# Four tiles of the per-layer embedding computed during the routing, the other four at the end of the expert stage

## The chip, the cores and the metric

The kernel runs on one core of a Trainium2 chip. Its time is the device time of one launch in microseconds (us). Three runs of the kernel before took 1029.37 to 1033.73 us, median 1030.36. The trace was taken in a further, profiled execution of the same kernel, which took 1031.45 us.

## The reference

One layer of a hybrid network on 1024 tokens of width 1024, in float32. The part that the change touches is what follows the mixers: the output projection, a mixture of 32 experts of which every token uses two, and an embedding that is added for each layer.

```python
x = x + jnp.concatenate([attn_out, ml_out], axis=-1) @ w_o[i]
x = x + _hier_moe(_rmsnorm(x, norm_ffn_g[i]), w_router_group[i], ..., w_gate_e[i], w_up_e[i], w_down_e[i])
hp = _rmsnorm(x, norm_ple_g[i])
x = x + (p[i] @ w_ple[i]) * jax.nn.sigmoid(hp @ w_ple_gate[i])
return _rmsnorm(x, final_norm_g)
...
def expert(args):                      # for the rows that the routing sent to expert e
    xb, e = args
    return (jax.nn.silu(xb @ w_g[e]) * (xb @ w_u[e])) @ w_d[e]
```

`p[i]` is 1024 x 256 and `w_ple` 256 x 1024. Their product, the per-layer embedding, depends on nothing that the layer computes, so that it can be made at any time before the last stage. In rows of 128 tokens it has eight tiles.

## The kernel before

Every large product is made from three products of rounded parts: a weight or activation is split into a high part (ScalarE copies it, rounding it) and a low part (VectorE subtracts), and `mm3` (L127 to L129) adds high x high, high x low and low x high. A split of 128 x 1024 elements thus takes one ScalarE and one VectorE instruction (L132, L133).

The stages in order are the mixers (up to about 430 us of the span), the output projection with the router's logits for eight row tiles (`out_tile`), the rest of the routing, the expert stage (`experts`), an overflow loop for experts with over 128 rows, and the final stage (gate by `w_ple_gate`, sum, norm).

In the output projection TensorE makes `wops` (the projection), transposes the result (`h2p`) and multiplies by the router's weights (`rps`). The sum x goes to `x2d` and the normalised rows go to `h2d` in DRAM, both on GpSimd's DMA queue. After the last tile comes what is called the gap of the routing here: counts (`cnt`), positions and two tables (`tab`) are worked out by VectorE and TensorE in turn, until the list `gidx` (L1017) tells which rows each expert takes. GpSimd then gathers the rows of the first two experts (L1149) into two buffers `xg` that ScalarE has filled before (L1200).

In the expert stage each step e gathers rows for expert e + 2, transposes and splits those of e + 1 (`xgp`, `xh`, `xl`), loads the weights of e + 3, multiplies expert e by its gate and up weights (`gups`, 24 matmuls of 128 x 512 in two halves), finishes e - 1 (transposes `ehp`, split `eht`, 12 + 12 matmuls `eyps`, eviction `ey`, scatter to `ybd`), and splits the weights of e + 1 and e. Each expert has two loads `rgu` for each half of gate and up (512 KB each) and one `rdn` of 1024 KB for down. They are issued by SyncE, in order, into a ring of nine raw buffers (4 KB or 8 KB a partition); a load waits until what stood in its buffer has been split. Split weights go into a second ring of buffers W.

A tile of the embedding (`ple_tile`) is two transposes `pps` of its input `pin`, a split of 128 x 256, twelve matmuls `pleps` of 128 x 512 and two evictions `pley`. Six tiles are made in the steps 14, 16, 18, 20, 22 and 24 (`PLE_AT`, L1235), in buffers of the raw ring that are given up for them (`retire`), one 8 KB buffer for two tiles. The weights `w_ple` are loaded in step 5 and split in steps 7 and 9. The seventh tile is made in `final_load`, ahead of the overflow loop, while the gate's weights `rpg` are loaded and split, and the eighth in `final`, after that loop. Instructions are ordered within an engine by a scheduler that takes priority, by place in the program, and dependences; each engine then runs its own list in order, and a semaphore wait holds up all that stands behind it on that engine.

Of the kernel before, what the change touches and what calls it, by code (L numbers as in the profile page):

```python
# [10 lines left out]
F32 = mybir.dt.float32  # L11
F32R = mybir.dt.float32r
# [8 lines left out]
P = 128  # L21
# [15 lines left out]
MLPRI = 800  # L37
PLE_LOAD = 5
PLE_W = (7, 9)
PLE_AT = (14, 16, 18, 20, 22, 24)  # L40
MAGIC = 12582912.0
# [18 lines left out]
class Kernel:  # L60
# [64 lines left out]
    def mm3(self, out, w_hi, w_lo, m_hi, m_lo, start, stop):  # L125
        nc = self.nc
        nc.tensor.matmul(out, w_hi, m_hi, start=start, stop=False)  # L127
        nc.tensor.matmul(out, w_hi, m_lo, start=False, stop=False)  # L128
        nc.tensor.matmul(out, w_lo, m_hi, start=False, stop=stop)  # L129

# [734 lines left out]
    def out_tile(self, i, gb, before):  # L865
# [14 lines left out]
        def mm(c, lo_k, hi_k):  # L880
            s = slice(c * 512, (c + 1) * 512)
            for k in range(lo_k, hi_k):
                self.mm3(ps[c], hi[:, k], lo[:, k], self.wo[k][:, 0, s], self.wo[k][:, 1, s], k == 0, k == KT - 1)

# [318 lines left out]
    def experts(self, gu3):  # L1203
        col = lambda t, e: t[:, e:e + 1]
        xg = [self.moe_gather(col(self.gidx, e)) for e in range(2)]
        with self.tc.issue_after(self.gathered.ins):
            self.raws[3] = gu3, self.load_gu(3, 1, self.nc.gpsimd), self.load_dn(3)
        x, gu, h, dn = {0: self.moe_x(xg[0])}, {0: self.first[0]}, {}, {0: self.first[1]}
        for e in range(N_EXP + 1):
            if e + 2 < N_EXP:  # L1210
                xg.append(self.moe_gather(col(self.gidx, e + 2)))
            if e + 1 < N_EXP:
                x[e + 1] = self.moe_x(xg[e + 1])
            if 4 <= e + 3 < N_EXP:
                self.raws[e + 3] = self.moe_load(e + 3)
            if e < N_EXP:
                h[e] = self.moe_gu(x.pop(e), gu.pop(e))
            if e:
                self.moe_y(h.pop(e - 1), dn.pop(e - 1), col(self.sidx, e - 1))
            if e + 1 < N_EXP:  # L1220
                with self.tc.issue_after(self.routed.ins):
                    gu[e + 1] = self.split_gu(self.raws[e + 1][:2])
            if 0 < e < N_EXP:
                dn[e] = self.split_w(self.raws.pop(e)[2:])
            if e == 4:
                with self.tc.issue_after(self.last_split[1]):
                    self.route_over()
                self.close("RT")
                self.open("PL", "right")
            if e == PLE_LOAD:  # L1230
                self.ple_load()
            if e in PLE_W:
                self.ple_weights(PLE_W.index(e))
            if e in PLE_AT:
                self.ple_tile(PLE_AT.index(e))  # L1235
            if e + 1 in PLE_AT[1:]:
                self.ple_in(PLE_AT.index(e + 1))

# [15 lines left out]
    def final_load(self):  # L1254
# [5 lines left out]
        raws = [self.R("rpg") for _ in range(4)]  # L1260
        for i in range(len(PLE_AT), NT):
            self.ple_in(i)
# [4 lines left out]
        with self.tc.issue_after(sa), self.tc.issue_after(sv):  # L1267
            self.wring, self.nw = wr, 0
            self.wgs = self.split_gate(raws[:1], 0)
            self.ple_tile(len(PLE_AT))  # L1270
            self.wgs += self.split_gate(raws[1:3], 2)
        self.rest = wr, raws[3:]
        self.fin = {}
# [5 lines left out]
    def ple_load(self):  # L1279
        self.plew = []  # L1280
        self.ple_raw = [self.ple_half(0)]
        self.pin, self.pw = {}, {}
        self.ple_in(0)

# [16 lines left out]
    def ple_tile(self, i):  # L1301
# [6 lines left out]
        py = self.po2("pleps")  # L1308
        n = i - len(PLE_AT)
        if n >= 0:  # L1310
            y = self.t("B", "pley", [P, D], bufs=2, tag="ey") if n % 2 else self.t("B", "pley", [P, D], tag=f"xg{n // 2 % 2}")
        else:
            if i % 2 == 0:
                pool, tag = self.retire()
                self.ples = self.t(pool, "ples", [P, 2 * D], tag=tag)
            y = self.ples[:, i % 2 * D:(i % 2 + 1) * D]
        for c in range(2):
# [50 lines left out]
    def final(self):  # L1368
# [5 lines left out]
        with self.tc.issue_after(self.fin[0][2].ins):  # L1374
# [5 lines left out]
            self.final_in(1)  # L1380
        rest = list(range(len(PLE_AT) + 1, NT))
        with ExitStack() as st:
# [39 lines left out]
    def run(self):  # L1422
# [13 lines left out]
        for i in range(NT):  # L1436
            end = self.out_tile(i, gb, end)
            if i == 1:
                self.raws[0] = self.moe_load(0)
            if i == 4:  # L1440
                list(self.route_tiles(0, 4))
                self.first = self.split_gu(self.raws[0][:2]), self.split_w(self.raws[0][2:])
            if i == 5:
                self.raws[1] = self.moe_load(1)
        rt = self.route_tiles(4, 7)
        next(rt)
        end()
        list(rt)
        gu2 = self.load_gu(2, 0)
        self.close("A3")  # L1450
# [3 lines left out]
        self.open("B", "left")  # L1454
        self.rring, self.nr = [("R2", f"R{i}") for i in range(4, 9)] + [self.rring[(self.nr + i) % 4] for i in range(4)], 0
        more = [("B", f"W{i}") for i in range(6, 9)]
        self.wring += more[:NW - 6]
        self.rring[5:5] = more[NW - 6:]
        self.raws[2] = gu2, self.load_gu(2, 1), self.load_dn(2)
        self.moe_setup()  # L1460
# [40 lines left out]
```

## Time and profile before

| | |
|---|---|
| median of 3 runs | 1030.36 us (1029.37 to 1033.73) |
| profiled execution | 1031.45 us, span 1029.7 us, mean granted TensorE clock 0.966 |
| TensorE (PE) busy | 953.9 us, 93% of the span |
| VectorE (DVE) busy | 805.8 us, 78% |
| ScalarE (ACT) busy | 666.7 us, 65% |
| SyncE's and ScalarE's DMA queue (q1) | 146.00 MB, 42.4% of 16 engines' span |
| GpSimd's DMA queue (q0) | 38.33 MB, 10.4% |

The span runs from the first to the last instruction; the shares are means over stages that differ much. The output projection runs from about 433 us, the gap from about 545 to 567, the experts up to about 909 and the final stage from 916. "PEclk" is the granted clock of TensorE, 1.00 being 2.4 GHz and 0.50 being 1.2 GHz. A release in brackets, as [5.77 <-DVE M L967], says how long the engine had been idle before the instruction and what ended that.

### The profile page before, as it was taken

How to read it: one execution, taken by the hardware profiler on the slowest of the kernel's cores; microseconds unless marked ns; L12 is line 12 of the kernel's file. 1: busy time of each engine (PE TensorE's matmuls, PEld its weight loads, DVE VectorE, ACT ScalarE, POOL GpSimd, SP SyncE). 2: the span in 40 equal slices, each digit the busy share in tenths (PEclk: the TensorE clock that was granted, in tenths of full speed). 3: DMA queues.
4: the chain of work that ended last, by engine and by line, in shares of the span. 5: the costliest groups of instructions: out<-in, count | busy, mean ns of one | idle time of the engine just before them, and what ended most of it. 6: DMA issues, size and time to landing. Idle time of an engine off the chain costs nothing. (4 is left out here: it accounts for less than half of the span.)

```text
span 1029.7 us, 16040 instructions
## 1 busy us (share of the span) xinstructions
PE 953.9 (93%) x5583; PEld 819.2 (80%) x5583; DVE 805.8 (78%) x1877; ACT 666.7 (65%) x1182; POOL 165.7 (16%) x213
## 2 busy tenths in 40 slices
PE   4999999998999999899995989999699999979996
PEld 4999999996788888688884867888588888858875
DVE  7759788367888989774747899998678889858885
ACT  5554766254788889763333877998578788755432
POOL 4000000101222322101013121222112112210000
PEclk9999999999999999899996998999899999989999
DMA  7230111310000001698348898999999999774541
GB/s 220 101 101 25 42 62 59 102 37 11 17 11 14 13 12 23 229 295 288 123 159 272 261 359 283 354 351 343 338 301 315 341 304 356 243 254 173 184 164 61
DMA packets 127360, 185.36 MB, mean 180 GB/s; under 512 B 19487, under 2 KB 105070, under 8 KB 123182
## 3 DMA queue, kind: packets, MB, share of 16 engines
q1 hardware_dynamic: 111502, 146.00, 42.4%
q0 software_dynamic: 15776, 38.33, 10.4%
q8 instruction: 44, 0.72, 0.3%
q14 instruction: 38, 0.31, 0.1%
HBM read 167.48 MB, written 33.59 MB: 195 GB/s over the span
## 5 line engine op out<-in xcount | busy, mean ns | idle before, releaser
L133 DVE TENSOR_TENSOR w<-rgu,w 128x1024 fp32r<-128x1024 f32 x128 | 155.1, 1227 | 32.8 <-ACT w L132 29.6
L132 ACT ACTIVATE w<-rgu 128x1024 fp32r<-128x1024 f32 x128 | 133.3, 1065 | 6.1 <-PE gups L129 3.3
L127 PE MATMUL inp<-hh,win 128*128 128x256 f32 x384 | 111.7, 291 | 0.0
L129 PE MATMUL inp<-hh,win 128*128 128x256 f32 x384 | 111.1, 290 | 0.5 <-DVE win L256 0.5
L128 PE MATMUL inp<-hl,win 128*128 128x256 f32 x384 | 111.4, 291 | 0.1
L127 PE MATMUL gups<-w,xh 128*128 128x512 f32 x256 | 103.8, 405 | 0.0
L128 PE MATMUL gups<-w,xh 128*128 128x512 f32 x256 | 102.0, 398 | 0.0
L129 PE MATMUL gups<-w,xl 128*128 128x512 f32 x256 | 101.2, 395 | 0.0
L133 DVE TENSOR_TENSOR w<-rdn,w 128x1024 fp32r<-128x1024 f32 x64 | 77.2, 1219 | 2.7 <-ACT w L132 1.9
L129 PEld LDWEIGHTS inp<-hh,win 128*128 128x128 f32 x384 | 74.6, 195 | 0.7 <-DVE win L256 0.7
L128 PEld LDWEIGHTS inp<-hl,win 128*128 128x128 f32 x384 | 74.6, 194 | 0.5 <-DVE hl L133 0.4
L127 PEld LDWEIGHTS inp<-hh,win 128*128 128x128 f32 x384 | 74.5, 194 | 0.3 <-ACT z L331 0.2
L132 ACT ACTIVATE w<-rdn 128x1024 fp32r<-128x1024 f32 x64 | 66.0, 1067 | 4.1 <-PE gups L129 3.7
L1149 POOL DMA_INDIRECT xg<-h2d,gidx x32 | 37.1, 1159 | 179.2 <-PE xgp L1159 145.8
L1188 ACT ACTIVATE ey<-eyps 128x512 f32<-128x512 f32 x64 | 38.2, 596 | 40.4 <-PE eyps L129 30.8
L705 PE MATMUL po<-pt,V 128*128 128x256 f32 x320 | 61.2, 307 | 0.9 <-ACT pt L132 0.5
L133 DVE TENSOR_TENSOR pt<-ptp,pt 128x512 fp32r<-128x512 f32 (+2 forms) x112 | 54.3, 491 | 7.3 <-ACT pt L132 5.7
L132 ACT ACTIVATE pt<-ptp 128x512 fp32r<-128x512 f32 (+2 forms) x112 | 48.1, 443 | 14.7 <-PE ptp L693 7.4
L127 PE MATMUL eyps<-w,eht 128*128 128x512 f32 x128 | 54.5, 426 | 2.4 <-ACT eht L132 2.3
L129 PEld LDWEIGHTS gups<-w,xl 128*128 128x128 f32 x256 | 48.3, 189 | 9.5
L128 PEld LDWEIGHTS gups<-w,xh 128*128 128x128 f32 x256 | 48.6, 190 | 9.1
L127 PEld LDWEIGHTS gups<-w,xh 128*128 128x128 f32 x256 | 48.7, 190 | 9.0 <-ACT xh L132 0.2
(392 smaller groups left out, 2633.2 us busy)
## 6 DMA issues: line engine op xcount, KB each, us to landing
rdn<-in_w_down_e_dram SPq DMA_DIRECT2D x32, 1024.0 KB, 8.9
rgu<-in_w_gate_e_dram SPq DMA_DIRECT2D x62, 512.0 KB, 11.5
rgu<-in_w_up_e_dram SPq DMA_DIRECT2D x62, 512.0 KB, 10.0
wraw<-in_w_in_dram SPq DMA_DIRECT2D x11, 512.0 KB, 5.4
x<-in_x_dram SPq DMA_DIRECT2D x8, 512.0 KB, 4.6
abw<-mlrows SPq DMA_DIRECT2D x8, 512.0 KB, 3.7
mixf<-mixd SPq DMA_DIRECT2D x8, 512.0 KB, 5.7
xres<-in_x_dram SPq DMA_DIRECT2D x8, 512.0 KB
```

The source lines that it names most:

```text
L127: nc.tensor.matmul(out, w_hi, m_hi, start=start, stop=False)
L128: nc.tensor.matmul(out, w_hi, m_lo, start=False, stop=False)
L129: nc.tensor.matmul(out, w_lo, m_hi, start=False, stop=stop)
L132: a = self.nc.scalar.activation(hi, src, AF.Copy)
L133: v = self.nc.vector.tensor_sub(lo, src, hi)
L705: nc.tensor.matmul(po, self.V[kt][:, h, :], pts[t - 1][:, w, u, :], start=(kt + w == 0), stop=(kt == 2 * j + 1 and w == 1))
L1149: self.gathered = self.nc.gpsimd.indirect_dma_start(out=xg, out_offset=None, in_=self.h2d, in_offset=bass.IndirectOffsetOnAxis(ap=gcol, ax ...
L1188: nc.scalar.activation(y[:, s], py[c], AF.Copy)
```

## The change

Four tiles (0 to 3) are made in the gap: `w_ple` (1 MB) and the four inputs (512 KB) are loaded during the output projection and the weights are split there, in buffers of the ring W; the products are evicted to buffers of the projection stage and stored to `pled` in DRAM by ScalarE's queue, one 512 KB store a tile. SyncE loads them again in steps 26 and 28, two tiles a load. Tiles 4 and 5 are made in `final_load`, tiles 6 and 7 in `final`; the weights are loaded a second time from step 20 on and split in steps 22 and 24. Further, expert 0's down weights are split in step 0 rather than in the projection, and expert 1's down load and all of expert 2's loads come after the projection's buffers are closed. `mm3` returns its last instruction, after which the early tiles may be issued, at a priority behind the routing.

```diff
-PLE_LOAD = 5
-PLE_W = (7, 9)
-PLE_AT = (14, 16, 18, 20, 22, 24)
+PLE_LOAD = 20
+PLE_W = (22, 24)
+N_EARLY = 4
+PLE_BACK = (26, 28)
...
-        x, gu, h, dn = {0: self.moe_x(xg[0])}, {0: self.first[0]}, {}, {0: self.first[1]}
+        x, gu, h, dn = {0: self.moe_x(xg[0])}, {0: self.first}, {}, {}
...
+            if e == 0:
+                with self.tc.issue_after(self.routed.ins):
+                    dn[0] = self.split_w(self.raws.pop(0)[2:])
...
-            if e in PLE_AT:
-                self.ple_tile(PLE_AT.index(e))
-            if e + 1 in PLE_AT[1:]:
-                self.ple_in(PLE_AT.index(e + 1))
+            if e in PLE_BACK:
+                self.ple_back(PLE_BACK.index(e))
...
+            self.ple_tile(N_EARLY)
             self.wgs += self.split_gate(raws[1:3], 2)
+            self.ple_tile(N_EARLY + 1)
...
+    def early_in(self):
+
+        raw = self.R("rple")
+        self.nc.sync.dma_start(raw, self.a["w_ple"][0].rearrange("(p k) n -> p (k n)", k=2))
+        self.early_w = raw
+
+    def early_p(self):
+        t = self.R("pins")
+        self.early_x = t.rearrange("p (i n) -> p i n", n=DE)
+        self.nc.sync.dma_start(self.early_x[:, 0:N_EARLY], self.a["p"][0, 0, 0:N_EARLY * P, :].rearrange("(i p) n -> p i n", p=P))
+
+    def early_split(self):
+        self.early_w = self.split_w([self.early_w])
+        self.pled = self.t("dr", "pled", [N_EARLY * P, D])
+
+    def early_tile(self, i):
+        nc = self.nc
+        pt = self.pT("pps")
+        for k in range(2):
+            nc.tensor.transpose(pt[:, k, :], self.early_x[:, i, k::2], self.ident)
+        ht = self.t("A3", "pht", [P, 2, 2, P], F32R, 2, "mixl")
+        self.split(ht[:, 0], ht[:, 1], pt[:, 0:2])
+        py = self.po2("pleps")
+        y = self.t("A3", "pley", [P, D], F32, 2, "mixh") if i % 3 else self.t("A3", "pley", [P, D], tag="mixf")
+        w = self.early_w
+        for c in range(2):
+            s = slice(c * 512, (c + 1) * 512)
+            for k in range(2):
+                self.mm3(py[c], ht[:, 0, k], ht[:, 1, k], w[k][0][:, s], w[k][1][:, s], k == 0, k == 1)
+            nc.scalar.activation(y[:, s], py[c], AF.Copy)
+        nc.scalar.dma_start(self.pled[i * P:(i + 1) * P, :], y)
+
+    def ple_back(self, n):
+        pool, tag = self.retire()
+        t = self.t(pool, "ples", [P, 2, D], tag=tag)
+        self.nc.sync.dma_start(t, self.pled[2 * n * P:2 * (n + 1) * P, :].rearrange("(i p) n -> p i n", p=P))
+        for i in range(2):
+            self.pw[2 * n + i] = t[:, i]
...
+            if i == 0:
+                self.early_in()
             if i == 1:
                 self.raws[0] = self.moe_load(0)
+            if i == 2:
+                self.early_split()
+                self.early_p()
             if i == 4:
                 list(self.route_tiles(0, 4))
-                self.first = self.split_gu(self.raws[0][:2]), self.split_w(self.raws[0][2:])
+                self.first = self.split_gu(self.raws[0][:2])
             if i == 5:
-                self.raws[1] = self.moe_load(1)
+                self.raws[1] = self.load_gu(1, 0), self.load_gu(1, 1)
         rt = self.route_tiles(4, 7)
         next(rt)
         end()
         list(rt)
-        gu2 = self.load_gu(2, 0)
+        with self.tc.issue_after(self.last_out.ins), self.tc.high_priority(-2000):
+            for i in range(N_EARLY):
+                self.early_tile(i)
         self.close("A3")
         list(self.route_tiles(7, 8))
         self.route_static()
         self.open("R2", "left")
         self.open("B", "left")
-        self.rring, self.nr = [("R2", f"R{i}") for i in range(4, 9)] + [self.rring[(self.nr + i) % 4] for i in range(4)], 0
+        self.rring, self.nr = [("R2", f"R{i}") for i in range(4, 9)] + [self.rring[i] for i in (3, 0, 1, 2)], 0
         more = [("B", f"W{i}") for i in range(6, 9)]
         self.wring += more[:NW - 6]
         self.rring[5:5] = more[NW - 6:]
-        self.raws[2] = gu2, self.load_gu(2, 1), self.load_dn(2)
+        self.raws[1] += self.load_dn(1),
+        self.raws[2] = self.moe_load(2)
```

Line numbers after the change are one to two higher than before it; L128 to L130 are L127 to L129 before.

TensorE at the end of the gap, before: the last table products (`tab`), then the transposes of the first gathered rows (`xgp`) and the first expert's products (`gups`).

```order
L1011 LDWEIGHTS Aoh
L1011 MATMUL tab<-Boh,Aoh 128x96
L1011 LDWEIGHTS Aoh
L1011 MATMUL tab<-Boh,Aoh 128x96
L1011 LDWEIGHTS Aoh
L1011 MATMUL tab<-Boh,Aoh 128x96
L1159 MATMUL xgp<-ident,xg_6431 128x128 x8
L127 MATMUL gups<-w,xh 128x512
L128 MATMUL gups<-w,xh 128x512
L1159 MATMUL xgp<-ident,xg_6432 128x128 x8
L129 MATMUL gups<-w,xl 128x512
```

The same place after the change; eighteen more `pleps` follow the last row here and then `xgp`.

```order
L1013 MATMUL tab<-Boh,Aoh 128x96
L128 MATMUL pleps<-w,pht 128x512
L129 MATMUL pleps<-w,pht 128x512
L130 MATMUL pleps<-w,pht 128x512
L128 MATMUL pleps<-w,pht 128x512
L1013 LDWEIGHTS Aoh
L1013 MATMUL tab<-Boh,Aoh 128x96
L1013 LDWEIGHTS Aoh
L1013 MATMUL tab<-Boh,Aoh 128x96
L129 MATMUL pleps<-w,pht 128x512
L130 MATMUL pleps<-w,pht 128x512
```

Two of the table products now stand behind four of the early tiles' products, and twenty of these stand ahead of `xgp`; 24 others stand earlier, ahead of `cnt`.

ScalarE in the gap, before: scaling of the normalised rows (`h`), the fill of the gather buffers (`xg`), two small steps of the routing weights, splits of expert 1's weights and of the gathered rows.

```order
L911 ACTIVATE h_6162<-h_6162,r_6165 128x512
L911 ACTIVATE h_6163<-h_6163,r_6165 128x512
L1200 ACTIVATE xg_6431<-io_f 128x1024
L1200 ACTIVATE xg_6432<-io_f 128x1024
L1031 ACTIVATE gd<-gd 128x32
L1037 ACTIVATE e_6445<-e_6445 128x8
L132 ACTIVATE w<-rgu 128x1024 x3
L132 ACTIVATE xh<-xgp 128x512 x4
```

After:

```order
L1317 ACTIVATE pley<-pleps 128x512
L1318 DMA pled<-pley 128x1024
L133 ACTIVATE w<-rgu 128x1024 x2
L1317 ACTIVATE pley<-pleps 128x512 x2
L1318 DMA pled<-pley 128x1024
L1202 ACTIVATE xg_6532<-io_f 128x1024
L1202 ACTIVATE xg_6533<-io_f 128x1024
L133 ACTIVATE w<-rdn 128x1024 x2
L133 ACTIVATE w<-rgu 128x1024
L133 ACTIVATE xh<-xgp 128x512 x4
L133 ACTIVATE w<-rgu 128x1024 x3
```

The fill of the gather buffers now stands behind the early tiles' evictions and stores and two weight splits; the small steps (`gd`, `e`) stand ahead of the first row shown. Expert 0's down split (`w<-rdn`) stands between the fill and the split of the gathered rows.

SyncE's queue after the last input of the output projection (`xres`), before: the second half of expert 2, two down loads, then expert 4.

```order
L872 DMA xres<-in_x_dram 128x1024 x2
L1115 DMA rgu<-in_w_gate_e_dram 128x4x256
L1115 DMA rgu<-in_w_up_e_dram 128x4x256
L1120 DMA rdn<-in_w_down_e_dram 128x2048 x2
L1115 DMA rgu<-in_w_gate_e_dram 128x4x256
L1115 DMA rgu<-in_w_up_e_dram 128x4x256
L1115 DMA rgu<-in_w_gate_e_dram 128x4x256
L1115 DMA rgu<-in_w_up_e_dram 128x4x256
L1115 DMA rgu<-in_w_gate_e_dram 128x4x256
```

After:

```order
L873 DMA xres<-in_x_dram 128x1024 x2
L1122 DMA rdn<-in_w_down_e_dram 128x2048 x2
L1117 DMA rgu<-in_w_gate_e_dram 128x4x256
L1117 DMA rgu<-in_w_up_e_dram 128x4x256
L1117 DMA rgu<-in_w_gate_e_dram 128x4x256
L1117 DMA rgu<-in_w_up_e_dram 128x4x256
L1122 DMA rdn<-in_w_down_e_dram 128x2048
L1117 DMA rgu<-in_w_gate_e_dram 128x4x256
L1117 DMA rgu<-in_w_up_e_dram 128x4x256
L1117 DMA rgu<-in_w_gate_e_dram 128x4x256
L1117 DMA rgu<-in_w_up_e_dram 128x4x256
```

The queue now begins with two down loads (of experts 3 and 1), both halves of expert 2 and its down load, and goes on with expert 4; the second half of expert 3 stays on GpSimd's queue.

## Rows read from the trace of the kernel before

**Rows 1.** Stretches: start:end and length, busy us (count) of each engine, clock, DMA share, GB/s.
```profile
562.00:567.00 5.00, 4.45 (x17) 3.55 (x18) 1.38 (x2) 1.51 (x3) 1.17 (x2) 0.50 0.97 322
...
540.00:715.00 175.00, 156.91 (x768) 128.93 (x767) 159.50 (x292) 133.12 (x191) 41.47 (x38) 0.92 0.92 316
...
640.00:715.00 75.00, 75.00 (x364) 61.88 (x363) 71.94 (x81) 66.44 (x96) 19.39 (x16) 1.00 0.99 346
...
715.00:893.00 178.00, 169.99 (x806) 139.63 (x805) 143.38 (x162) 142.37 (x207) 35.56 (x31) 0.97 0.95 323
...
860.00:880.00 20.00, 20.00 (x99) 16.49 (x98) 19.29 (x22) 18.58 (x28) 4.79 (x5) 1.00 1.05 370
```

**Rows 2.** Timeline of the routing gap: start, us, engine, line, operation, [idle <- releaser].
```profile
554.49 0.21 PE L970 MATMUL cnt<-M,upper 128*128 128x32 bf16 x1 [5.77 <-DVE M L967]
...
562.46 1.95 PE L1159 MATMUL xgp<-ident,xg 128*128 128x128 f32 x8 [6.21 <-DMA xg<-h2d,gidx]
...
551.18 1.99 ACT L1200 ACTIVATE xg<-io_f 128x1024 f32<-128x1024 f32 x2
...
563.59 0.60 ACT L132 ACTIVATE xh<-xgp 128x512 fp32r<-128x512 f32 x1 [3.37 <-PE xgp L1159]
...
556.73 0.19 DVE L1017 SCALAR_TENSOR_TENSOR gidx<-row,tab 128x32 int32<-128x32 f32 x1
...
557.84 1.10 POOL L1149 DMA_INDIRECT xg<-h2d,gidx  x1 [3.67 <-DVE e21d L1039]
```

**Rows 3.** Timeline of TensorE and VectorE in expert steps with and without a tile.
```profile
702.32 0.39 PE L1179 MATMUL ehp<-ident,eh 128*128 128x128 f32 x2
...
711.81 0.39 PE L1179 MATMUL ehp<-ident,eh 128*128 128x128 f32 x2
...
714.42 0.42 DVE L133 TENSOR_TENSOR eht<-pps,eht 128x256 fp32r<-128x256 f32 x1
...
724.33 0.39 PE L1179 MATMUL ehp<-ident,eh 128*128 128x128 f32 x2
...
734.63 0.39 PE L1179 MATMUL ehp<-ident,eh 128*128 128x128 f32 x2
...
742.51 0.67 PE L1305 MATMUL pps<-ident,pin 128*128 128x128 f32 x2 [7.49 <-DMA pin<-in_p_dram]
...
757.28 0.39 PE L1179 MATMUL ehp<-ident,eh 128*128 128x128 f32 x2
```

**Rows 4.** Timeline of SyncE's DMA queue: weight loads of experts.
```profile
540.23 0.38 SPq L1115 DMA_DIRECT2D rgu<-in_w_gate_e_dram  x1
...
676.89 0.35 SPq L1120 DMA_DIRECT2D rdn<-in_w_down_e_dram  x1
...
719.29 1.99 SPq L1120 DMA_DIRECT2D rdn<-in_w_down_e_dram  x1
```

**Rows 5.** Timeline of ScalarE: splits of expert weights and the last expert's.
```profile
715.76 1.06 ACT L132 ACTIVATE w<-rgu 128x1024 fp32r<-128x1024 f32 x1 [2.81 <-DMA rgu<-in_w_up_e_dram]
...
887.62 1.05 ACT L132 ACTIVATE w<-rgu 128x1024 fp32r<-128x1024 f32 x1
...
906.13 0.38 ACT L132 ACTIVATE eht<-ehp 128x256 fp32r<-128x256 f32 x1
```

**Rows 6.** Timeline of ScalarE at the start of the output projection.
```profile
441.31 1.04 ACT L132 ACTIVATE mixh<-mixf 128x1024 fp32r<-128x1024 f32 x1
...
448.85 0.60 ACT L888 ACTIVATE wops<-xres 128x512 f32<-128x512 f32 x1 [6.50 <-issue]
```

**Rows 7.** Timeline of TensorE around the overflow loop and the first final tile.
```profile
916.75 0.70 PE L1305 MATMUL pps<-ident,pin 128*128 128x128 f32 x2 [4.17 <-issue]
...
922.74 0.60 PE L1363 MATMUL fp<-ident,fxy 128*128 128x128 f32 x4
...
924.07 0.50 PE L127 MATMUL fps<-w,xh 128*128 128x512 f32 x1 [0.74 <-ACT xh L132]
```

**Rows 8.** Costliest groups of the page: busy, mean ns | idle before, releaser.
```profile
L1188 ACT ACTIVATE ey<-eyps 128x512 f32<-128x512 f32 x64 | 38.2, 596 | 40.4 <-PE eyps L129 30.8
```

More of the change, by code (lines that the diff above doesn't have):

```diff
@@ L128, in mm3 @@
         nc.tensor.matmul(out, w_hi, m_lo, start=False, stop=False)
-        nc.tensor.matmul(out, w_lo, m_hi, start=False, stop=stop)
+        return nc.tensor.matmul(out, w_lo, m_hi, start=False, stop=stop)
     def split(self, hi, lo, src):
@@ L882, in mm @@
             for k in range(lo_k, hi_k):
-                self.mm3(ps[c], hi[:, k], lo[:, k], self.wo[k][:, 0, s], self.wo[k][:, 1, s], k == 0, k == KT - 1)
+                self.last_out = self.mm3(ps[c], hi[:, k], lo[:, k], self.wo[k][:, 0, s], self.wo[k][:, 1, s], k == 0,
+                                         k == KT - 1)
         def norm(c):
@@ L1260, in final_load @@
         raws = [self.R("rpg") for _ in range(4)]
-        for i in range(len(PLE_AT), NT):
+        for i in range(N_EARLY, NT):
             self.ple_in(i)
@@ L1269, in final_load @@
             self.wgs = self.split_gate(raws[:1], 0)
-            self.ple_tile(len(PLE_AT))
+            self.ple_tile(N_EARLY)
             self.wgs += self.split_gate(raws[1:3], 2)
+            self.ple_tile(N_EARLY + 1)
         self.rest = wr, raws[3:]
@@ L1282, in ple_load @@
         self.pin, self.pw = {}, {}
-        self.ple_in(0)
+    def early_in(self):
[31 more added lines that the diff above has]
+            self.pw[2 * n + i] = t[:, i]
     def ple_in(self, i):
@@ L1308, in ple_tile @@
         py = self.po2("pleps")
[L1309 to L1316, printed above, removed]
+        n = i - N_EARLY
+        y = self.t("B", "pley", [P, D], bufs=2, tag="ey") if n % 2 else self.t("B", "pley", [P, D], tag=f"xg{n // 2 % 2}")
         for c in range(2):
@@ L1380, in final @@
             self.final_in(1)
-        rest = list(range(len(PLE_AT) + 1, NT))
+        rest = list(range(N_EARLY + 2, NT))
         with ExitStack() as st:
```

## The prediction

> **What bounds the kernel now.** I read first, by stretches, the busy time of each engine beside the DMA share and the bytes moved [rows 1]. From 640 to 715 us TensorE is busy 75.00 of 75.00 us and, in the same stretch, the 16 DMA engines are busy 0.99 of it and move 346 GB/s. From 715 to 893 us it is 169.99 of 178.00 us and 0.95 at 323 GB/s. So in the expert stage two things are nearly full at once, and taking work from one of them shows how far away the other is. Dividing the GB/s by the share gives what the queues would move when never idle: 316/0.92 = 343, 346/0.99 = 349, 323/0.95 = 340, 370/1.05 = 352. All four lie near 346, which I take for the stream of expert weights.
>
> The second view is the timeline of one expert [rows 3]: the step of an expert without a per-layer tile is 711.81 - 702.32 = 9.49 us of TensorE, one with a tile 724.33 - 711.81 = 12.52, so a tile costs 3.03. Over 13 experts, from 757.28 to the stage's end near 893, with four tiles, this makes 13 x 9.49 + 4 x 3.03 = 135.5 us: the time that passes. There TensorE sets the pace. The third view is SyncE's queue [rows 4]: the down loads of four successive experts are issued from 676.89 to 719.29, 10.6 us apart, which is 3.67 MB (three weights of 1 MB in binary measure, and the gathered rows) at 346 GB/s. So while the stream is behind, an expert costs 10.6 us of DMA against 9.49 us of TensorE. Before the change the tiles fill that difference.
>
> The fourth view is the waits of the splits [rows 5]: ScalarE waits 2.81 us for the up half of an expert at 715.76; at that point the stream is what is late. The fifth is the gap of the routing [rows 2]: TensorE waits 5.77 us for VectorE's routing and 6.21 us for the first gathered rows.
>
> **The change part by part.** The sum is made against the profiled execution's own 1031.45 us, 1.09 over the median of 1030.36.
>
> A. Start of the output projection. The diff's early tiles make the scheduler place the small transposes of the first row tile ahead of the second tile's projection, which needs the split of the second mixed tile; that split stands behind squares and copies on ScalarE. One split is 1.04 us and one eviction 0.60 [rows 6], ScalarE before had 6.50 us of nothing to do there. About two splits' worth: +2 us. The nearest rows bound it by 0 (the order costs nothing) and +5 (most of that idle stretch is needed).
>
> B. The gap. Before, the gather is issued at 557.84 and the first expert's rows are split from 563.59 [rows 2], 5.75 us later. Of the change's 48 early matmuls on TensorE, 24 stand ahead of the last counting matmul; they go into the 5.77 us wait, which they fill (24 x 0.23 = 5.5, from 12 matmuls in a tile of 2.75 to 3.03 us). Three more VectorE subtractions of 0.42 us [rows 3] stand ahead of the gather's index: +1.3. Four early matmuls stand ahead of the last two table matmuls: +0.9. Twenty follow, so the last early matmul ends near 556.73 + 1.3 + 0.9 + 20 x 0.23 = 563.5, less the 0.5 us that the index follows the table: 563. ScalarE then runs in order two weight splits, which take over the early weight's buffers and wait for that last matmul, two evictions, a store and only then the fill of the gather buffers (L1200, 1.99 us for two), for which both gathers wait: 563 + 2 x 1.06 [rows 5] + 2 x 0.60 [rows 8] + 1.0 = 567.3. Against 557.84 that is +9.5. Bounds: +5 if half of the ScalarE queue is done sooner than this, +12 if the evictions wait on buffers for their stores. I take +9.5. Nothing hides it, since gather, transposes and the first expert form one chain. Expert 0's down split, which moves from the projection stage to here, stands on ScalarE between that fill and the split of the gathered rows, and its buffers are free when the fourth store has landed, near 570; with three splits of 1.06 it ends about 573, when the rows come (567.3 + 5.75), and costs nothing unless that store is late, when each us of it is one of the start.
>
> C. Experts. Six tiles go: five of 3.03, and the one in the step 734.63 to 757.28, which is 22.65 - 9.49 = 13.16, as TensorE waited 7.49 us for its input and then ran slowly [rows 3]. Together 28.3 us of TensorE. The evictions of those tiles go from ScalarE too, which is not the bound.
>
> D. End. Before, one tile follows the last expert, and one follows the overflow loop. Afterwards two and two. The first extra tile falls into the 4.17 us for which TensorE has no instruction before 916.75 [rows 7]: nothing. The second stands between 922.74 and 924.07, where 0.74 us of waiting hides part of its 2.75: +2.0.
>
> TensorE alone would give +2 + 9.5 - 28.3 + 2.0 = -14.8: 1016.7.
>
> E. The weight stream. This decides whether C arrives. Before, SyncE issued the second half of expert 2 at 540.23 [rows 4], having already sent expert 1's down weight and expert 2's first half before the gap. Afterwards its first weight load in the gap reuses the buffer next to the early input, and waits for the last early transposes, about 557: 17 us later. From 540 to 715, 316 x 175 = 55.3 MB were moved. The change adds 2.1 MB that used to move before (the two loads just named) and 2.1 MB of stores of the early tiles; it takes away 1.2 MB of tile weights and inputs that go elsewhere in time, and some 3 MB (activations and expert 3's first half, on GpSimd's queue) still move before 557. So again 55.3 MB are wanted before the half that was split at 715.76, at 346 GB/s: 160 us from 557, or 717; with A's 2 us it is 719 to 720. From there to the last expert's first half there are sixteen experts at 10.4 to 10.6 us, 168 us, and 2.1 MB for the late load of the tile weights and the first return of stored tiles, 6 us. It arrives at about 893.5 where its split before ran at 887.62 [rows 5]. Before, TensorE was behind there, and the last down transposes' copy ran only at 906.13, 18.5 us later. A stage that waits for its weights has only a plain step of 9.49 left: 903.0. That is -3.1, and with D's +2.0 the sum is -1.1: own time 1030.3. Per expert 10.4 rather than 10.6 takes off 3 more at most, the slow side adds as much; I take -1.8, 1029.6, which on the median's scale is 1028.5.
>
> The Trainium skill's page "DMA: Bandwidth & Descriptors", section "Where 436 GB/s comes from", says that between HBM and on-chip memory the HBM side binds at about 358 GB/s a core, but reports 425 GB/s for a large load with the neighbour idle. At 358 an estimate gives 10.3 us for an expert's 3.67 MB and hence this forecast; at 425 it would be 8.6, less than TensorE's step, and hence the first rival. The quotients near 346 speak for the lower figure in this stream.
>
> **The rivals.**
> 1. The stream keeps up. For it speaks the stretch 860 to 880 with 370 GB/s [rows 1]; at that rate an expert is 9.9 us and sixteen of them gain 11 us. Against it the share there is 1.05, so that it is no more than 352 per full share, and the 10.6 us spacing. With TensorE alone bounding it is 1016.7 own; half-way, 1024.
> 2. Slower: the stream starts late and nothing returns it. SyncE's queue runs in order, and in the gap one load waits for each stored tile to land. If the third store, issued near 561, holds the queue until 565, and what was sent before that does not keep the DMA engines busy, the stream starts from 565 rather than 557: +8 on E, 1038. For it speaks that several loads stand behind these waits; against it that 3 MB released at 557 are worth 9 us. It decides if the last expert's first half is split after about 897.
> 3. The gap's clock. From 562 to 567 TensorE ran at a granted 0.50, the 1.2 GHz level, after its waits [rows 1, 2]. If the early tiles keep the clock up there, its 4.45 us busy become half: up to -2.2 more, and as much again if A's stretch behaves so: 1026 to 1027. Against it: the gap only moves, since TensorE will wait again between the early tiles' end and the later gather.
>
> **How the numbers follow.** The forecast has 0.44, rival 1 0.30, rival 2 0.18, rival 3 0.08. A difference of under 0.5%, about 5 us, is what a measurement of this kernel can't tell from none. The forecast's own range on the median's scale is 1023.5 to 1034, from A's 0 to 5, B's 5 to 12 as far as the stream doesn't cover them, and 3 us of the stream either way; of its 0.44, 0.06 lies below 1025, 0.32 within and 0.06 above. Rival 1 gives 0.28 faster and 0.02 within, rival 2 0.16 slower and 0.02 within, rival 3 0.03 faster and 0.05 within. Together faster 0.37, same 0.41, slower 0.22. The range goes from rival 1's lower end to most of rival 2: 1016 to 1037.
>
> **What would show it.** Right: the first gather about 10 us later; expert steps without tiles at 10 to 10.7 us, with TensorE or its splits waiting for weights, the clock at times below full, DMA share near 0.99 from 557 on; the copy of 906.13 at 900 to 906; the end +2. Wrong: expert steps at 9.5 throughout (rival 1), or the last first half after 897 (rival 2). A gather at 558 would refute B; loads in the gap at 540 would refute E.

## The result and the profile after

The changed kernel takes 1047.81 us in the median of 4 runs (1044.6 to 1049.21), beside 1030.13 us for the kernel before on the same chip (4 runs, 1029.37 to 1033.73). The ratio is 1.016 with a 95% interval of 1.0127 to 1.0194: slower by 1.6%, where no measurable change was forecast, and above the end of the range at 1037. The profiled execution has a span of 1047.4 us, 17.7 over the 1029.7 of before; both profiled executions are 1.3 to 1.4 us above these medians.

Three instants divide this difference: the first and the last of the down transposes (`ehp`), which bound the stage of the experts, and the end. Before they are at 578.62 and 905.44 in a span of 1029.7 (with the gap's first counting product, `cnt`, which is used further down); after at 598.61 and 920.29 in 1047.4 (the first and last row of the fence of down transposes below).

```profile
546.10 0.21 PE L970 MATMUL cnt<-M,upper 128*128 128x96 bf16 x1
...
578.62 0.39 PE L1179 MATMUL ehp<-ident,eh 128*128 128x128 f32 x2
...
905.44 0.39 PE L1179 MATMUL ehp<-ident,eh 128*128 128x128 f32 x2
```

| | before | after | difference | forecast |
|---|---|---|---|---|
| start to the first `ehp` | 578.62 | 598.61 | +20.0 | +11.5 |
| first to last `ehp` | 326.82 | 321.68 | -5.1 | -14.6 |
| last `ehp` to the end | 124.26 | 127.11 | +2.8 | +2.0 |

(The second forecast is -3.1, for the copy behind the last `ehp`, less the +11.5 at the start; -28.3 of TensorE's work were to go from this stretch.)

By stretches (columns as in [rows 1]), the gap and the two stretches of the expert stage:

```profile
545.00:562.00 17.00, 15.40 (x98) 12.80 (x98) 14.13 (x83) 6.72 (x14) 3.12 (x5) 1.00 0.29 91
...
640.00:715.00 75.00, 75.00 (x365) 62.09 (x364) 69.50 (x87) 64.03 (x90) 17.36 (x14) 0.97 0.94 320
...
715.00:893.00 178.00, 164.01 (x772) 134.31 (x771) 146.89 (x165) 137.46 (x199) 35.52 (x32) 0.96 0.99 343
```

In the gap TensorE is now busy 15.40 of 17.00 us at the full clock. In the expert stage, though, it is busy 164.01 of 178.00 us from 715 on, against 169.99 in [rows 1], while the DMA share has risen from 0.95 to 0.99 and the rate from 323 to 343 GB/s. The freed time of TensorE became idle time, and the stream of weights is full.

The gap after, engine by engine (start, duration, engine, line, operation, and in brackets the idle time before it and what ended it):

```profile
559.75 0.18 PE L972 MATMUL cnt<-M,upper 128*128 128x32 bf16 x1 [1.09 <-DVE M L969]
...
578.29 1.94 PE L1161 MATMUL xgp<-ident,xg 128*128 128x128 f32 x8 [11.97 <-DMA xg<-h2d,gidx]
...
565.67 2.00 ACT L133 ACTIVATE w<-rgu 128x1024 fp32r<-128x1024 f32 x2 [1.46 <-PE pleps L130]
...
567.58 1.06 ACT L1317 ACTIVATE pley<-pleps 128x512 f32<-128x512 f32 x2
...
569.05 2.00 ACT L1202 ACTIVATE xg<-io_f 128x1024 f32<-128x1024 f32 x2 [0.40 <-ACT pley L1317]
...
577.35 2.00 ACT L133 ACTIVATE w<-rdn 128x1024 fp32r<-128x1024 f32 x2 [6.30 <-DMA pled<-pley]
...
580.21 1.06 ACT L133 ACTIVATE xh<-xgp 128x512 fp32r<-128x512 f32 x2
...
570.39 1.10 POOL L1151 DMA_INDIRECT xg<-h2d,gidx  x1 [11.11 <-ACT xg L1202]
```

Against [rows 2]: the counting product waits 1.09 us where it waited 5.77, so the early tiles did fill that wait. The gathered rows' transposes come at 578.29 instead of 562.46, and their wait has grown from 6.21 to 11.97 us. ScalarE shows why: two weight splits behind the last early product, evictions, then the fill of the gather buffers at 569.05 rather than 551.18; GpSimd's gather, which had been idle for 11.11 us, waits for that fill. Two smaller losses come behind it. The gathered rows are longer on their way: the first `xgp` comes 7.90 us after the gather's issue, where it came 4.62 after it in [rows 2]. And expert 0's down split waits 6.30 us for the fourth store (`pled`), with the split of the gathered rows (`xh`, 580.21) behind it in ScalarE's queue, now 1.92 us after the first `xgp` and not 1.13.

Down transposes on TensorE, the steps of the stage, and the longest of its waits:

```profile
598.61 0.39 PE L1181 MATMUL ehp<-ident,eh 128*128 128x128 f32 x2
...
750.73 0.39 PE L1181 MATMUL ehp<-ident,eh 128*128 128x128 f32 x2
...
760.72 0.39 PE L1181 MATMUL ehp<-ident,eh 128*128 128x128 f32 x2
...
804.96 0.39 PE L1181 MATMUL ehp<-ident,eh 128*128 128x128 f32 x2
...
815.21 0.80 PE L128 MATMUL eyps<-w,eht 128*128 128x512 f32 x1 [8.48 <-ACT eht L133]
...
824.99 0.39 PE L1181 MATMUL ehp<-ident,eh 128*128 128x128 f32 x2
...
920.29 0.39 PE L1181 MATMUL ehp<-ident,eh 128*128 128x128 f32 x2
```

The first fifteen steps, to 750.73, take 152.1 us, where the same steps before took 156.0, from 578.62 to 734.63 [rows 3], with one tile of 3.03 among them: up to here the change gives what was computed. Then come steps of 13.83 us (760.72 on), 20.03 (804.96 on) and 15.04 (892.95 on), in which TensorE waits for the copy `eht`, 8.48 us at 815.21. The copy is late because ScalarE, working in order, stands ahead of it at a split whose weights have not landed:

```profile
788.25 1.06 ACT L133 ACTIVATE w<-rgu 128x1024 fp32r<-128x1024 f32 x1 [3.36 <-DMA rgu<-in_w_up_e_dram]
...
813.56 1.06 ACT L133 ACTIVATE wp<-rple 128x1024 fp32r<-128x1024 f32 x1 [7.88 <-DMA rple<-in_w_ple_dram]
...
890.03 1.06 ACT L133 ACTIVATE w<-rgu 128x1024 fp32r<-128x1024 f32 x1 [4.98 <-DMA rgu<-in_w_up_e_dram]
...
898.95 1.06 ACT L133 ACTIVATE w<-rgu 128x1024 fp32r<-128x1024 f32 x1 [1.13 <-DMA rgu<-in_w_up_e_dram]
...
920.99 0.38 ACT L133 ACTIVATE eht<-ehp 128x256 fp32r<-128x256 f32 x1
```

One such wait was there before ([rows 5], 2.81 us); now there are, besides four of 0.48 to 1.68, waits of 3.36, 7.88 (for the second copy of the tiles' weights), 4.98 and 1.13 us, the last at the first split of the last expert, 22.0 us ahead of the last copy at 920.99. At the end of the kernel the two tiles behind the overflow loop put the first final product off: 944.62 is 24.3 us behind the last `ehp`, 924.07 in [rows 7] was 18.6 behind it; of these 5.7 us 2.8 are left at the end.

```profile
944.62 0.39 PE L128 MATMUL fps<-w,xh 128*128 128x512 f32 x1
```

### The profile page after: what moved, and what is told of

It is laid out like the page before. It is cut to its first block, busy times and chain, and to the rows that moved or that the text cites. A ratio compares the mean times of both kernels' runs of the same rounds, so it can differ in the third digit from the quotient of the medians.

```text
span 1047.4 us, 16033 instructions
## 1 busy us (share of the span) xinstructions
PE 960.0 (92%) x5583; PEld 823.0 (79%) x5583; DVE 807.4 (77%) x1879; ACT 668.9 (64%) x1184; POOL 164.8 (16%) x213
## 5 line engine op out<-in xcount | busy, mean ns | idle before, releaser
L128 PE MATMUL inp<-hh,win 128*128 128x256 f32 x384 | 111.4, 291 | 0.0
L129 PE MATMUL inp<-hl,win 128*128 128x256 f32 x384 | 111.1, 290 | 0.1
L130 PE MATMUL inp<-hh,win 128*128 128x256 f32 x384 | 110.7, 289 | 0.5 <-DVE win L257 0.5
L128 PE MATMUL gups<-w,xh 128*128 128x512 f32 x256 | 104.2, 407 | 0.6 <-ACT xh L133 0.6
L129 PE MATMUL gups<-w,xh 128*128 128x512 f32 x256 | 102.8, 402 | 0.0
L130 PE MATMUL gups<-w,xl 128*128 128x512 f32 x256 | 101.7, 397 | 0.0
L134 DVE TENSOR_TENSOR w<-rdn,w 128x1024 fp32r<-128x1024 f32 x64 | 77.0, 1217 | 11.5 <-ACT w L133 11.3
L130 PEld LDWEIGHTS inp<-hh,win 128*128 128x128 f32 x384 | 74.2, 193 | 0.7 <-DVE win L257 0.7
L129 PEld LDWEIGHTS inp<-hl,win 128*128 128x128 f32 x384 | 74.2, 193 | 0.5 <-DVE hl L134 0.4
L128 PEld LDWEIGHTS inp<-hh,win 128*128 128x128 f32 x384 | 74.1, 193 | 0.3 <-ACT z L332 0.2
L128 PE MATMUL eyps<-w,eht 128*128 128x512 f32 x128 | 56.0, 438 | 18.7 <-ACT eht L133 18.6
L1161 PE MATMUL xgp<-ident,xg 128*128 128x128 f32 x256 | 41.4, 289 | 18.4 <-DMA xg<-h2d,gidx 13.3
L128 PEld LDWEIGHTS gups<-w,xh 128*128 128x128 f32 x256 | 48.9, 191 | 10.0 <-ACT xh L133 1.0
L130 PEld LDWEIGHTS gups<-w,xl 128*128 128x128 f32 x256 | 48.9, 191 | 9.8
```

Source lines behind the costliest of these rows:

```text
L130: return nc.tensor.matmul(out, w_lo, m_hi, start=False, stop=stop)
L134: v = self.nc.vector.tensor_sub(lo, src, hi)
L1161: self.nc.tensor.transpose(pt[:, k, :], xg[:, 4 * b + k::KT], self.ident)
```

## The experiments

Two theories were set against each other. Theory R: the stage is paced by the stream of weights, whose ring of nine raw buffers is full before the experts start; a late start is therefore passed on whole, and TensorE's freed time turns into waits. Rival S: TensorE and the order of the engines' queues set the pace. A third, M: the loads that were moved behind the gap are the loss.

**Only a later start (b_late, b_late2).** The kernel before, with ScalarE's fill repeated:

```diff
-        for x in self.xgs:
+        for x in self.xgs * 8:        # b_late; * 14 in b_late2
```

> Kernel before with sixteen fills of the gather buffers on ScalarE instead of two (fourteen repeat the same values), so that the first gather is issued about 10 us later and nothing else changes. Theory R (the ring of nine raw buffers is full before the experts start, so a late start moves the weight stream with it): +8 to +10 us, 1038 to 1040, first down transposes near 588. The prediction's own step E (the stream runs on through the gap and only its bytes decide): 0 to +3, 1030 to 1033.

> Kernel before with twenty-eight fills of the gather buffers. With sixteen the first down transposes ran at 583.8 (+5.2) and the time was 0.5 to 1.2% more; twelve more fills put them at about 595 to 597 (+17). Theory R (a late start is passed on whole): +16 to +19, 1046 to 1050, that is as much as the whole change costs. If the stream, which starts at 540 here and not at 559, makes use of the time: +5 to +9, 1035 to 1040.

Measured: ratios 1.0085 (1.0055 to 1.0116) and 1.0161 (1.0126 to 1.0196). The medians moved by 7.4 us (1031.37 to 1038.75) and 16.9 (1031.53 to 1048.41); both are what R said, and neither fits a stream that runs on. In the profile of b_late the start moved by 5.2 us only, since the stages ahead of the gap took 2.7 us less in that execution (first `cnt` at 543.45 for 546.10); from there to the first `ehp` it is 7.9 us longer than before. In b_late2 that way is 19.2 us longer, the start moved by 19.4 us, the last `ehp` by 20.1, the span by 21.2 (the profiled execution is the slowest of its four). First and last `ehp` of b_late2:

```profile
597.97 0.39 PE L1179 MATMUL ehp<-ident,eh 128*128 128x128 f32 x2
...
925.53 0.39 PE L1179 MATMUL ehp<-ident,eh 128*128 128x128 f32 x2
```

So a late start is passed on, by the medians about nine tenths of it, with a stream that starts at 540 as before. Why is shown by two stretches of b_late2 and by SyncE's queue in it, with the longest of its waits (us in total, times, longest):

```profile
540.00:560.00 20.00, 9.91 (x67) 8.17 (x65) 15.49 (x89) 12.52 (x18) 3.13 (x5) 0.73 0.81 286
...
560.00:580.00 20.00, 0.00 (x0) 0.00 (x0) 1.78 (x7) 20.00 (x24) 2.42 (x3) 0.50 0.03 3
```

```profile
541.47 2.49 SPq L1120 DMA_DIRECT2D rdn<-in_w_down_e_dram  x2
...
581.52 0.38 SPq L1115 DMA_DIRECT2D rgu<-in_w_gate_e_dram  x1
```

```profile
SPq L1115 <- DVE w L133: 118.8, 25, 37.6
```

After the two down loads at 541.47 SyncE issues nothing until 581.52, and from 560 to 580 us the DMA engines are busy 0.03 of the time: the ring is full, and a buffer comes free only when an expert's weights are split (`w`, whose last part is VectorE's), for which SyncE waits 37.6 us here. A late start by itself, of the size that the change has, costs what the change costs. That alone would fit S too, since a stage paced by TensorE would also end later by what it starts later; the next two tests part the theories.

**The tiles out of the stage (b_notiles).**

```diff
-            if e in PLE_AT:
-                self.ple_tile(PLE_AT.index(e))
-            if e + 1 in PLE_AT[1:]:
-                self.ple_in(PLE_AT.index(e + 1))
+            if e in PLE_AT[::2]:
+                self.retire()
```

> Kernel before without tiles 0 to 5 of the per-layer embedding and their inputs (the last stage multiplies by tile 6 in their place); the three ring buffers are given up as before. Removes 28 us of TensorE from the expert stage. Theory R: -5 to -9 us, 1021 to 1025, with waits for weights in their place. Rival S: -25 to -28, 1002 to 1005.

Measured: 0.9932 (0.9905 to 0.9958), 7 us as R said, and not 28. ScalarE's splits in it, and one stretch:

```profile
738.11 1.06 ACT L132 ACTIVATE w<-rgu 128x1024 fp32r<-128x1024 f32 x1 [3.31 <-DMA rgu<-in_w_up_e_dram]
...
744.84 2.00 ACT L132 ACTIVATE w<-rgu 128x1024 fp32r<-128x1024 f32 x2 [2.77 <-DMA rgu<-in_w_up_e_dram]
...
788.27 1.06 ACT L132 ACTIVATE w<-rgu 128x1024 fp32r<-128x1024 f32 x1 [6.10 <-DMA rgu<-in_w_up_e_dram]
```

```profile
715.00:860.00 145.00, 132.09 (x609) 107.45 (x608) 117.51 (x132) 111.69 (x160) 32.96 (x26) 0.95 0.99 341
```

Waits of 3.31, 2.77 and 6.10 us for up weights stand in the place of the tiles; the DMA engines are busy 0.99 of the stretch at 341 GB/s, TensorE 132.09 of 145.00 us. This is the size that term C could have, whatever is done with the tiles.

**A lighter stream (b_halfdn, a_halfdn).** Both kernels with half of the down weights (both parts of the split read that half):

```diff
-        self.nc.sync.dma_start(raw, self.weight("w_down_e", e).rearrange("(p k) n -> p (k n)", k=2))
+        self.nc.sync.dma_start(raw[:, 0:D], self.weight("w_down_e", e).rearrange("(p k) n -> p (k n)", k=2)[:, 0:D])
```

> Kernel before with half of every expert's down weights loaded (512 KB instead of 1024; both halves of the product use the same half). The stream gets 14% lighter, the engines' work is the same. Theory R: the waits for weights and for the tile input at 742 us go, TensorE sets the pace alone, about -10 us: 1018 to 1022. Rival (the stream did not bind): 1028 to 1030.

> Changed kernel with the same half of the down weights. Theory R: all the late waits of the expert stage go (some 23 us), steps of 9.5 us to the end, 1022 to 1028, and the distance to the kernel before with the same edit shrinks from 17 to between 3 and 7 us: late start +20 less 18 of tiles, +3 at the end. Rival S (order of the engines' queues holds the stage): over 1038, the waits at ScalarE's splits stay.

Measured: 0.9902 (0.9877 to 0.9927), 1020.19 us, and 0.9917 (0.989 to 0.9944), 1020.86 us. The distance between the two kernels goes from 17 us to under one by the medians and 2.5 by the profiled spans, which is less than R's 3 to 7 (and a_halfdn is a little under R's 1022), for a reason that the last lines of this part show. The same stretch in b_halfdn, then in a_halfdn:

```profile
715.00:860.00 145.00, 145.00 (x700) 119.29 (x699) 122.86 (x140) 121.59 (x178) 31.51 (x28) 1.00 0.87 284
```

```profile
715.00:860.00 145.00, 145.00 (x705) 120.03 (x703) 135.96 (x153) 128.10 (x185) 35.81 (x31) 1.00 0.98 336
```

TensorE is busy without a break in both, so no wait for weights is left in this stretch; in a_halfdn the DMA engines are at 0.98 even so, at 336 GB/s, since the steps without tiles ask for that much. From the first to the last `ehp` the changed kernel now takes 298.6 us, the other 315.0: 16.4 us of the tiles' 18 (six at 3.03) arrive once the stream does not bind. This is the test that decides against S: only the bytes are fewer, and the change costs next to nothing. The order is not quite the same either: in a_halfdn the second load of the tiles' weights stands at 645 us and their splits at 652 and 671, not at 804, 814 and 838 as in the changed kernel. That this is not what helped is shown by a_wple5 below, which has them at 648, 655 and 678 with the full stream, and is no faster than the changed kernel. The first and last `ehp` of a_halfdn:

```profile
591.65 0.39 PE L1182 MATMUL ehp<-ident,eh 128*128 128x128 f32 x2
...
890.21 0.39 PE L1182 MATMUL ehp<-ident,eh 128*128 128x128 f32 x2
```

Its start, 591.65, is 7 us earlier than in the changed kernel. Of these 4.0 stand ahead of the gap (first `cnt` at 545.77 for 549.73); 0.8 are the way of the gathered rows (7.06 us for 7.90), and 2.2 come behind that, where the down split waits 3.99 us for the store and not 6.30.

**The tile weights' second load earlier (a_wple5).**

```diff
-PLE_LOAD = 20
-PLE_W = (22, 24)
+PLE_LOAD = 5
+PLE_W = (7, 9)
```

> Changed kernel with the second load of the tile weights in step 5 and their splits in steps 7 and 9, as before, instead of 20, 22 and 24. Theory R (1 MB moves to where the stream had room at 640 to 660 us, the 7.88 us wait of ScalarE's split at 813 is only where the lateness shows): -2 to -4 us, 1044 to 1046. Rival S (that wait in ScalarE's queue is a loss of its own): -9 to -11, 1037 to 1039.

Measured: 1.0179 (1.0152 to 1.0205), no gain, which is outside both expectations, by less from R's. The 7.88 us wait is gone; splits of the experts wait instead, eight times for 2.1 to 3.4 us and once for 4.46:

```profile
890.38 1.06 ACT L133 ACTIVATE w<-rgu 128x1024 fp32r<-128x1024 f32 x1 [4.46 <-DMA rgu<-in_w_up_e_dram]
```

The longest wait on the list was not a cause, only the place where the lateness of the stream showed.

**What of the early tiles costs (a_nostore, a_noearly).** In a_nostore the stores and the loads in steps 26 and 28 are left out, in a_noearly the early tiles altogether (the early load and split of their weights and the load of their inputs stay there):

```diff
-        nc.scalar.dma_start(self.pled[i * P:(i + 1) * P, :], y)     # a_nostore
...
-            for i in range(N_EARLY):                                # a_noearly
-                self.early_tile(i)
```

> Changed kernel in which the four early tiles are computed and evicted, but neither stored nor loaded again (the last stage multiplies by tile 4 in their place). Takes away 4.2 MB of DMA and the wait of expert 0's down split for the last store. Theory R: first down transposes 3 to 5 us earlier than 598.6, the late waits for weights shorter by the 6 us that 2.1 MB take, total 1038 to 1043. Rival M: 1045 to 1048, since the early products in front of the gather and the moved loads stay.

> Changed kernel without the work of the four early tiles: no early transposes, products, stores, and no loads of them in steps 26 and 28 (the last stage multiplies by tile 4 in their place; two ring buffers are given up as in the changed kernel). What stays is the later issue of expert 1's down load and of expert 2's loads, the tile weights' second load and two more tiles at the end. Theory R (late start and stream bytes): first down transposes within 4 us of before (579 to 583), 4.2 MB less of DMA, total 1026 to 1034. Rival M (the loads that were moved past the gap are the loss): the start stays near 590 or later and the total is over 1038.

Measured: a_nostore 1.0073 (1.0053 to 1.0094), 1038.6, at the lower end of what R said. Its start is at 591.50, 7.1 us earlier than with the stores, where R said 3 to 5. Not all of this is the stores: 1.9 stand ahead of the gap (first `cnt` at 547.80 for 549.73) and 1.2 between that and the gather; the gathered rows take 7.90 us on their way, as they do with the stores. The other 3.9 come behind them, as expert 0's down split follows the fill at once: from the first `xgp` to the first `ehp` it is 16.4 us here, 20.3 with the stores and 16.2 in the kernel before.

```profile
567.79 1.99 ACT L133 ACTIVATE w<-rdn 128x1024 fp32r<-128x1024 f32 x2
...
575.13 1.94 PE L1161 MATMUL xgp<-ident,xg 128*128 128x128 f32 x8 [10.96 <-DMA xg<-h2d,gidx]
...
591.50 0.39 PE L1181 MATMUL ehp<-ident,eh 128*128 128x128 f32 x2
```

a_noearly gave 1.0047 (1.003 to 1.0064), a little over R's range, and its start missed both: 587.29 rather than 579 to 583. Of these 8.7 us 7.0 stand ahead of the gap (first `cnt` at 553.05 for 546.10), part of them in a wait of 2.08 us, with a clock of 0.91 from 480 to 500 us where the two main kernels have 1.00:

```profile
487.00 1.31 PE L901 MATMUL rps<-wr,h2t 128*128 128x36 f32 x8 [2.08 <-ACT h2t L897]
...
553.05 0.21 PE L972 MATMUL cnt<-M,upper 128*128 128x96 bf16 x1
...
587.29 0.39 PE L1181 MATMUL ehp<-ident,eh 128*128 128x128 f32 x2
...
905.35 0.39 PE L1181 MATMUL ehp<-ident,eh 128*128 128x128 f32 x2
```

M is not borne out: with the moved loads left as they are, less than 5 of the 17 us remain, and from the gap on the start is only 1.7 us later than before. What M may have of the loss is in the way of the gathered rows: 4.69 us in this kernel, whose moved loads go out from 547 on and ahead of the gather, and 7.90 in the changed kernel, where they wait for the last early transposes and go out beside it. No run parts this from the rest.

Taken together, the start's lateness, the 7 us of b_notiles and the 2.8 us at the end add up in each of these kernels: 20.0 - 7 + 2.8 = +15.8 for the change (measured +16.5, the ratio times 1030), 12.9 - 7 + 2.8 = +8.7 for a_nostore (+7.5), 8.7 - 7 + 2.8 = +4.5 for a_noearly (+4.8). The -7 is a round value for all three: in the profiles the stage from first to last `ehp` is 5.1, 10.4 and 8.8 us shorter than before, so that the store and the loads back seem to cost some 5 us in the stage besides what they cost at the start.

**A faster kernel (b_pins, b_pins_at).** The wait of 7.49 us for a tile's input in [rows 3] needs no tile moved:

```diff
-            if e + 1 in PLE_AT[1:]:
-                self.ple_in(PLE_AT.index(e + 1))
+            if e + 2 in PLE_AT[1:]:
+                self.ple_in(PLE_AT.index(e + 2))
```

> Kernel before with the inputs of the per-layer tiles issued two steps ahead rather than one. Takes away the 7.49 us wait and the slow clock behind it. Theory R (after the middle of the stage TensorE and the stream are both nearly full, so that freed TensorE time turns into waits for weights): -3 to -5 us, 1025 to 1027. Rival S (TensorE sets the pace): -10, 1020.

> Kernel before with the tiles' inputs issued two steps ahead (as in b_pins) and its six tiles two steps later, in steps 16 to 26. Theory R: TensorE waits for weights least where tiles stand; where the stream is late (715 to 790 us) the work moved away leaves waits, later the stream has room: 0 to -2 against b_pins, 1024 to 1027. If TensorE sets the pace: no change against b_pins.

Measured: b_pins 0.9949 (0.9934 to 0.9965), 1026.37 us, the fastest complete kernel here; b_pins_at 0.9976 (0.9959 to 0.9993), 1028.68, worse than b_pins (the two intervals just touch) and so against both expectations; the cause stays open. In b_pins:

```profile
735.30 0.39 PE L1179 MATMUL ehp<-ident,eh 128*128 128x128 f32 x2
...
747.83 0.39 PE L1179 MATMUL ehp<-ident,eh 128*128 128x128 f32 x2
...
771.21 0.39 PE L1179 MATMUL ehp<-ident,eh 128*128 128x128 f32 x2
```

The step that took 22.65 us ([rows 3], from 734.63) is now 12.53, but the step from 771.21 takes 13.33 where it holds no tile: ScalarE waits 2.66 us for up weights at 767.63 and TensorE 1.32 us for the copy behind it, so that part of the 10 us comes back as waits for weights.

## Why the prediction was wrong

A held. The third tile's first transposes come 3.6 us later (463.01 for 459.39), of which 1.4 stood before the projection's first product, in the stage ahead; the +2 is right, and so is its reason: the second tile's product waits 0.47 us for the split `mixh` at 452.22, and the clock is 0.83 from 450 to 460 us, where it was 1.00.

B was right down to the fill behind the evictions, and mis-sized behind it. Forecast was +9.5 for the gather; it was issued 12.55 us later (570.39 for 557.84), which is 8.9 without A's 3.6. But B let nothing come behind that, and the first `ehp` is 16.4 us later without A's part. Of the other 7.5 us, 3.3 are the longer way of the gathered rows (7.90 us for 4.62): they are not due to the stores, as a_nostore has the same 7.90, and point to the weight loads of the gap that went out beside them, with the DMA engines at 1.05 from 570 to 580 us; in a_noearly, whose loads went out ahead of the gather, it is 4.69. The last 4.2 come behind the rows. There the sentence that expert 0's down split "costs nothing unless that store is late" applies: the store was late, by the 6.30 us of ScalarE's wait, and a_nostore puts this part at 3.9 us.

C's 28.3 us of TensorE were taken out as computed, and E was right that they would not arrive: 5 did, and b_notiles says 7 without any of the rest. D's +2.0 was +2.8.

Two steps of E failed, by 12 to 13 us each. The first is "160 us from 557, or 717": it lets the stream run on without a stop, so that the half that was split at 715.76 comes at 719 to 720. The first weight load of the gap did go out at 558.70, close to the 557. But the same half, the first of expert 16, was split at 732.48, without a wait for it:

```profile
732.48 1.06 ACT L133 ACTIVATE w<-rgu 128x1024 fp32r<-128x1024 f32 x1
```

The stream stops when the ring is full, and the ring empties at the pace of the experts, which started late:

```profile
590.00:600.00 10.00, 8.71 (x45) 7.09 (x44) 7.71 (x11) 8.57 (x12) 0.98 (x1) 1.00 0.87 293
...
600.00:610.00 10.00, 10.00 (x50) 8.31 (x49) 9.44 (x11) 8.93 (x14) 2.01 (x2) 1.00 0.75 217
```

At that time (after the first experts' splits, columns as in [rows 1]) the share is 0.87 and 0.75; in the kernel before it is 0.85 and 0.73 from 570 to 590, the same stop 20 us earlier. So the lateness of the start, which E took to be covered by that of the stream, was the stream's lateness too.

The second is "A stage that waits for its weights has only a plain step of 9.49 left." From the first split of the last expert to the last copy there are 22.0 us after and 21.8 before:

```profile
884.36 1.06 ACT L132 ACTIVATE w<-rgu 128x1024 fp32r<-128x1024 f32 x1
```

884.36 to 906.13 is 21.8 us; in b_pins and b_notiles the same two stand 21.8 and 21.9 us apart, and in all twelve kernels between 21.1 and 22.5. It is the depth of the pipeline, since an expert's first split, its products and its down transposes stand in successive steps, and no backlog that a late stream could use up. (The row at 887.62 in [rows 5] is that expert's second split, and not the first as the prediction had it.) This alone is 12 us: by its own arrival at 893.5 and 21.8 us behind it the forecast would have been +11, slower.

That the arrival itself, 898.95, is only 5 us later than E's 893.5 is luck. From the half at 715.76 to the last expert's first half E counts sixteen experts; the rows have fifteen, from expert 16 to expert 31, in either kernel. With fifteen, E's own rates give about 883, 16 us too early: the 13 of the stream's stop, and 3 that the fifteen took longer (166.5 us, with the late loads, where E's rates give 163.5). The error in the count hid the larger part of the first one.

Rival 2 had the sign and the test (a last half after 897), but not the reason: SyncE's queue was held in the gap, 9.36 and 4.70 us at two loads, yet the DMA engines had enough to do then (0.99 and 1.05 of the time from 560 to 580 us), and b_late2, where the stream is as early as before, loses as much.

```profile
558.70 1.77 SPq L1122 DMA_DIRECT2D rdn<-in_w_down_e_dram  x2
...
562.41 9.36 SPq L1117 DMA_DIRECT2D rgu<-in_w_gate_e_dram  x1
...
571.81 4.70 SPq L1117 DMA_DIRECT2D rgu<-in_w_up_e_dram  x1
```

Rival 1 is refuted by the steps above, rival 3 was right on the gap itself, which ran at 1.00, but the clock fell to 0.51 in the longer wait behind it (570 to 580 us) and was 0.64 at the first experts' products (580 to 590 us), as it was before (560 to 570), so that nothing was gained.

## What to carry to other kernels

Before work is moved out of a stage, leave it out there and time that: 28 us of the busiest engine were worth 7, as the stream beside it was 0.95 to 0.99 full. Work that is moved into a gap is free only if nothing of it stands ahead of the gap's chain on any engine; here one fill, behind two splits and two evictions in ScalarE's queue, set the largest part of the late start of a stage that passes on nearly every microsecond of it. A buffer ring that is full ahead of a stage ties the stream to the stage's start, and the work left after the last load is the pipeline's depth, to be read from the rows. An arrival that is forecast by counting steps has to be checked by counting them in the rows.

## What was not expected of the hardware

The bytes moved per full DMA share were nearly the same in all kernels, whatever the mix: 341/0.99 = 344, 336/0.98 = 343, 343/0.99 = 346, 320/0.94 = 340, and 284/0.87 = 326 in the lightest. None of the long stretches shown here goes over 346 GB/s; so the rate of about 358 GB/s in the Trainium skill's page "DMA: Bandwidth & Descriptors" (section "Where 436 GB/s comes from") was approached here, and the 425 GB/s that it names for a load of 16 MB was not, in a stream of 512 KB and 1 MB loads of one core.
